# Attention beside a state-space scan on one core: some of the next unit's preparation steps move from between the scores to between the value products

## The chip, the cores and the metric

The kernel runs on one core of one Trainium2 chip (trn2). The metric is the device time of one execution in microseconds (us), the median of several runs. In the text PE is the matmul engine, DVE the vector engine, ACT the scalar engine, POOL the GpSimd engine and SP the queue that issues most DMAs. "Score" is q times k, "value product" is the weights times v.

## What is computed

One layer of a transformer that mixes attention with a state-space scan, for 2048 latent and 256 context tokens. The part that the change touches is the attention: 8 query heads on 2 key/value heads of size 64; latent queries attend to 2048 latent and 512 cached context keys, context queries to 256 keys.

```python
def block_attention(q, k, v):
    ...
    def one_block(q_blk):
        s = jnp.einsum("bqkgd,bskd->bkgqs", q_blk, k, preferred_element_type=jnp.float32) * scale
        p = jax.nn.softmax(s, axis=-1).astype(v.dtype)
        return jnp.einsum("bkgqs,bskd->bqkgd", p, v)
```

The state-space mixer (per direction a complex diagonal scan over the tokens) is independent of the attention; its work is put between the attention's instructions. Projections come before both, a gated projection and a feed-forward network after both.

## The kernel before

The attention is cut into **units**: one kv head, one pair of query heads, and 512 latent queries (16 latent units of 20 key blocks each) or 256 context queries (4 context units of 2 key blocks). A unit goes through its key blocks in **slots**, one for each block of 128 keys. In a slot, `scores` does four matmuls (L266, L267, two for each head, in the rounded format fp32r) and one exponential on ACT (L269). `values` does the value products of a slot (L283, two matmuls in full fp32, which the trace shows as four records) and adds p into a running sum for the denominators, on POOL (L296) or, for every fourth slot of a latent unit, the last of its group, on DVE (L293). Slots go in **groups of four**. `attend` writes the scores of group g+1 and then the values of group g, so PE alternates between a score phase (16 matmuls) and a value phase (16 records).

The exponential needs the row maximum of the scores beforehand. So while a unit runs, `prep` prepares the **next** one, as a generator whose every `yield` is one **step**: transposes of q (L218) and their split (L219, L222), then 40 maxima steps for a latent unit, each of one matmul (L197, 512 keys by 128 queries into one PSUM tile named `m`) and one reduction on DVE (L198, `mx<-m`); when a head's maxima are complete, a small reduction (L204), ACT and a transpose (L205, L210) put their negative into the operand `ql`. The tile `m` has three buffers, and everything that needs a scratch PSUM tile takes its turn on them: maxima, transposes, the denominators' sums (L317), the matmuls of the scan.

Inside `slot` the counter `st["q"]` grows by `st["per"]`, the steps still to do divided by 19.5, and a step is run for each whole number. In the windows of a latent unit whose successor is a latent unit `per` is 52 / 19.5 = 2.67, so two or three steps follow the scores of each slot. In the first three windows a context unit is prepared as well and `per` is 68 / 19.5 = 3.49.

After the values of a group come three things, in this order: a step of `finish` for a unit that has ended (among them an addition L312 and, one group on, the matmuls L317; another group on, the multiplication L335, which waits for a DMA), and one step of the generator `Sg`, which runs the scan. `Sg` also gets one step after the scores of each slot. Its five steps for a group mean that the scan's DVE work falls behind the values: per scan unit either three products and sums with the rotation table (L1032, L1033, L1034, here **s**), or the scan itself (L1040), or two products (L1047, L1048, here **r**), or one difference (L1052). The scan's matmuls (L1012, L982, L984, 48 short ones) fall into the score phase of about one group in five.

On PE and DVE the order of the program text is the order of execution: the attention is written inside

```python
    with tc.manual_schedule(engines={mybir.EngineType.PE, mybir.EngineType.DVE}):
        fin = attend(B, Sg)
```

The other engines and queues are ordered by the scheduler. The functions that the change touches, with the lines of the profile:

Of the kernel before, what the change touches and what calls it, by code (L numbers as in the profile page):

```python
# [48 lines left out]
def build(nc, tc, I, O):  # L49
# [76 lines left out]
    def run(g):  # L126
        for _ in g:
            pass
# [130 lines left out]
    def scores(ui, j):  # L259
        kv, tok, nq, k0, k1, pr_ = units[ui]  # L260
        khl, kho = KK[kv, k0]
        st = X["pst"].tile([128, 2, 512], F32, name="st")
        kc = slice(j * 128, (j + 1) * 128)
        for h in range(2):
            qh, ql = QT[ui][h]
            PE.matmul(st[:, h, 0:nq], khl[:, kc], qh[:, 0:nq], start=True, stop=False)  # L266
            PE.matmul(st[:, h, 0:nq], kho[:, kc], ql[:, 0:nq], start=False, stop=True)  # L267
        p = X["wk"].tile([128, 2, 512], F32, name="p", bufs=11)
        S.activation(p[:, :, 0:nq], st[:, :, 0:nq], AF.Exp, scale=0.125)  # L269
        pts[ui, j] = p  # L270
# [3 lines left out]
    def values(ui, j):  # L274
        kv, tok, nq, k0, k1, pr_ = units[ui]
        nk = k1 - k0
        if j == 0:
            PV[ui] = X["ppv"].tile([128, 512], F32, name="pv")
            ACC[ui] = {}
        pv, acc = PV[ui], ACC[ui]  # L280
        p = pts.pop((ui, j))
        for h in range(2):
            PE.matmul(pv[64 * h:64 * h + 64, 0:nq], X["vall"][:, k0 + j, 64 * kv:64 * kv + 64], p[:, h, 0:nq],  # L283
                      start=j == 0, stop=j == nk - 1)
        if nk <= 4:
            e = "v"
        elif ui + 1 == len(units):
            e = "v" if j % 3 == 2 or j > 16 else "g"
        else:
            e = "v" if j in VJ else "g"  # L290
        if e in acc:
            if e == "v":
                V.tensor_add(acc[e][:, :, 0:nq], acc[e][:, :, 0:nq], p[:, :, 0:nq])  # L293
            else:
                for h in range(2):
                    G.tensor_add(acc[e][:, h, 0:nq], acc[e][:, h, 0:nq], p[:, h, 0:nq])  # L296
        else:
            acc[e] = p
        if j == nk - 1:
            pvs = X["wk"].tile([128, 512], F32, name="pvs", bufs=2)  # L300
            S.copy(pvs[:, 0:nq], pv[:, 0:nq])
            PEND.append((ui, pvs, acc))
# [4 lines left out]
    def finish():  # L307
        ui, pvs, acc = PEND.pop(0)
        kv, tok, nq, k0, k1, pr_ = units[ui]
        a = acc["v"]  # L310
        if "g" in acc:
            V.tensor_add(a, a, acc["g"])  # L312
        if ui + 1 < len(units):
            yield
        sT = X["pmx"].tile([128, 512], F32, name="m")
        for h in range(2):
            PE.matmul(sT[64 * h:64 * h + 64, 0:nq], ones, a[:, h, 0:nq], start=True, stop=True)  # L317
        rT = X["wk"].tile([128, 512], F32, name="rT", bufs=2)
        if ui + 1 == len(units):
            V.reciprocal(rT[:, 0:nq], sT[:, 0:nq])  # L320
        else:
            S.copy(rT[:, 0:nq], sT[:, 0:nq])
            nc.sync.dma_start(out=rs_scr[ui, :, 0:nq], in_=rT[0:128:64, 0:nq])
            w = 2 * nq // 128
            rr = X["wk"].tile([128, 8], F32, name="rr", bufs=2)[:, 0:w]
            for h in range(2):
                nc.sync.dma_start(out=rr[64 * h:64 * h + 64], in_=rs_scr[ui, h, 0:nq].rearrange("(p w) -> p w", p=64))
            yield
            V.reciprocal(rr, rr)
            for h in range(2):  # L330
                nc.sync.dma_start(out=rr_scr[ui, h, 0:nq].rearrange("(p w) -> p w", p=64), in_=rr[64 * h:64 * h + 64])
            for h in range(2):
                nc.sync.dma_start(out=rT[64 * h:64 * h + 64, 0:nq], in_=rr_scr[ui, h:h + 1, 0:nq].to_broadcast([64, nq]))
        yield
        V.tensor_mul(pvs[:, 0:nq], pvs[:, 0:nq], rT[:, 0:nq])  # L335
        nc.sync.dma_start(out=a_scr[256 * kv + 128 * pr_:256 * kv + 128 * pr_ + 128, tok:tok + nq], in_=pvs[:, 0:nq])
# [3 lines left out]
    def prep_steps(ui):  # L340
        kv, tok, nq, k0, k1, pr_ = units[ui]
        n = 2 * (nq // 128) * ((k1 - k0 + 3) // 4) + 12
        first = next(i for i, u_ in enumerate(units) if (u_[0], u_[3]) == (kv, k0))
        return n + (1 + (k1 - k0 + 3) // 4 if ui == first else 0)

    def attend(B, Sg):
        groups = []
        for ui, u_ in enumerate(units):
            js = [(ui, j) for j in range(u_[4] - u_[3])]
            groups += [js[i:i + GROUP] for i in range(0, len(js), GROUP)]  # L350
        st = dict(ready=0, q=0.0, per=0.0, goal=1, s=0.0)
        fin = []

        def step():
            st["ready"] = next(B) or st["ready"]

        def slot(ui, j):
            while st["ready"] < ui:
                step()
            lat = units[ui][2] > 256  # L360
            if lat and not j:
                st["goal"] = min(ui + (2 if ui + 1 < 2 * len(cu) else 1), len(units) - 1)
                st["per"] = sum(prep_steps(i) for i in range(st["ready"] + 1, st["goal"] + 1)) / 19.5
                st["q"] = 0.0
            scores(ui, j)
            st["q"] += st["per"] if lat else 0.0
            while st["q"] >= 1.0:
                st["q"] -= 1.0
                if st["ready"] < st["goal"]:
                    step()  # L370
            if lat:
                X["pos"] = "p"
                next(Sg, None)

        for s_ in groups[0]:
            slot(*s_)
        for gi, g in enumerate(groups):
            if gi + 1 < len(groups):
                for s_ in groups[gi + 1]:
                    slot(*s_)  # L380
            for s_ in g:
                values(*s_)
            for f in list(fin):
                if next(f, "end") == "end":
                    fin.remove(f)
            if gi + 1 < len(groups) and len(groups[gi + 1]) > 2:
                X["pos"] = "v"
                next(Sg, None)
            if PEND:
                fin.append(finish())  # L390
        run(Sg)
        return fin
# [754 lines left out]
    with tc.manual_schedule(engines={mybir.EngineType.PE, mybir.EngineType.DVE}):  # L1147
        fin = attend(B, Sg)
# [569 lines left out]
```

## Time and profile before

| what | value |
|---|---|
| median of 3 runs | 3324.7 us (3320.79 to 3324.88) |
| the profiled execution's own time | 3312.73 us |
| its span, from first to last instruction | 3310.9 us |
| PE busy | 92% of the span |
| DVE busy | 77% |
| POOL busy | 57% |
| ACT busy | 41% |
| latent attention, from 476.88 us to 1419.73 us | 942.85 us |

A busy PE is not a PE at its peak: the ends of its matmuls are modelled, and waits that are shorter than a matmul's tail do not show as idle time. What a wait costs is therefore read from the starts of neighbouring matmuls. Times inside the trace are counted from the span's start.

### The profile page before, as it was taken

What the parts mean: (1) busy time and instruction counts of PE and PEld (TensorE: products, weight loads), DVE (VectorE), ACT (ScalarE), POOL (GpSimd) and SP (SyncE); (2) the same over time, 40 slices, a digit from 0 to 9 for tenths busy, and PEclk for the clock granted to TensorE, in tenths of its full rate; (3) what the DMA queues carried; (4) which work ended last, traced back from release to release, by engine and by line L of the source; (5) the groups of instructions that cost most, each with busy time, mean ns of one, the idle gap of its engine ahead of it and who ended that gap; (6) DMA issues with size and microseconds to landing.
All of it is one profiled execution on the core that took longest, in us unless ns stands there. A gap on an engine that the chain in (4) does not pass through costs nothing. (4 is left out here: it accounts for less than half of the span.)

```text
span 3310.9 us, 46264 instructions
## 1 busy us (share of the span) xinstructions
PE 3059.0 (92%) x16087; PEld 2468.7 (75%) x16087; DVE 2547.8 (77%) x3444; ACT 1341.8 (41%) x2378; POOL 1888.8 (57%) x1373
## 2 busy tenths in 40 slices
PE   7898889999999999996997999999999999989897
PEld 5787665555655565565776999999989998868686
DVE  4899766777777787667878877887787877577887
ACT  4333334444444444544555333443343334232332
POOL 3777526655775785774435544554455555354675
PEclk9999999999999999998998999999999999999899
DMA  7565452323333322214565444444434445658653
GB/s 264 181 198 191 145 133 55 89 71 87 85 81 90 81 75 52 65 60 138 184 184 184 134 120 121 129 136 118 121 106 130 122 127 185 155 151 198 179 199 137
DMA packets 515379, 435.19 MB, mean 131 GB/s; under 512 B 106374, under 2 KB 449454, under 8 KB 515148
## 3 DMA queue, kind: packets, MB, share of 16 engines
q1 hardware_dynamic: 498060, 400.57, 40.1%
q0 software_dynamic: 5184, 18.88, 3.3%
q10 hardware_dynamic: 11904, 12.82, 1.2%
q8 instruction: 127, 2.08, 0.3%
q14 instruction: 104, 0.85, 0.1%
HBM read 279.37 MB, written 143.73 MB: 128 GB/s over the span
## 5 line engine op out<-in xcount | busy, mean ns | idle before, releaser
L296 POOL TENSOR_TENSOR p<-p 128x512 f32<-128x512 f32 x442 | 647.0, 1502 | 286.7 <-PE pv L283 185.7
L89 POOL TENSOR_TENSOR op<-wr,op 128x512 fp32r<-128x512 f32 (+1 forms) x297 | 416.4, 1409 | 413.5 <-ACT op L88 373.9
L95 PE MATMUL o<-h,op 128*128 128x384 f32 x1848 | 621.3, 336 | 18.3 <-DVE h L89 17.2
L94 PE MATMUL o<-h,op 128*128 128x384 f32 x1848 | 621.0, 336 | 16.4 <-ACT h L88 15.8
L96 PE MATMUL o<-h,op 128*128 128x384 f32 x1848 | 620.2, 336 | 0.0
L198 DVE TENSOR_REDUCE mx<-m 128x1 f32<-128x512 f32 (+1 forms) x656 | 404.8, 675 | 134.6 <-PE m L197 133.3
L269 ACT ACTIVATE p<-st 128x1024 f32<-128x1024 f32 (+1 forms) x328 | 331.4, 1016 | 245.5 <-PE st L267 236.3
L88 ACT CAST op<-sw 128x512 fp32r<-128x512 f32 (+1 forms) x381 | 232.5, 612 | 328.7 <-PE o L95 257.0
L95 PEld LDWEIGHTS o<-h,op 128*128 128x128 f32 x1848 | 349.2, 189 | 20.8 <-DVE h L89 19.3
L94 PEld LDWEIGHTS o<-h,op 128*128 128x128 f32 x1848 | 349.0, 189 | 18.2 <-ACT h L88 17.2
L96 PEld LDWEIGHTS o<-h,op 128*128 128x128 f32 x1848 | 349.2, 189 | 0.0
L89 POOL TENSOR_TENSOR op<-sw,op 128x512 fp32r<-128x512 f32 (+1 forms) x177 | 259.4, 1469 | 118.4 <-ACT op L88 118.3
L88 ACT CAST op<-wr 128x512 fp32r<-128x512 f32 (+1 forms) x333 | 198.9, 607 | 244.7 <-PE o L95 162.7
L283 PE MATMUL pv<-p,vall 128*64 128x512 f32 (+1 forms) x1312 | 296.4, 593 | 0.0
L95 PE MATMUL o<-fvm,op 128*128 128x512 f32 x693 | 277.7, 401 | 19.9 <-POOL fvm L89 10.5
L94 PE MATMUL o<-fvm,op 128*128 128x512 f32 x693 | 276.7, 400 | 11.3 <-ACT fvm L88 9.6
L266 PE MATMUL st<-qh,khl 128*128 128x512 f32 (+1 forms) x656 | 277.6, 424 | 9.8 <-ACT p L269 8.8
L96 PE MATMUL o<-fvm,op 128*128 128x512 f32 x693 | 274.4, 396 | 0.0
L267 PE MATMUL st<-ql,kho 128*128 128x512 f32 (+1 forms) x656 | 259.4, 396 | 0.0
L197 PE MATMUL m<-khl,qh 128*128 128x512 f32 (+1 forms) x656 | 230.0, 422 | 30.5 <-DVE mx L198 20.2
L283 PEld LDWEIGHTS pv<-p,vall 128*64 128x64 f32 x1312 | 86.8, 136 | 158.2 <-issue 155.0
L197 PEld LDWEIGHTS m<-khl,qh 128*128 128x128 f32 x656 | 124.3, 191 | 103.5 <-DVE mx L198 67.7
(314 smaller groups left out, 6302.2 us busy)
## 6 DMA issues: line engine op xcount, KB each, us to landing
wr<-w_ffn_in SPq DMA_DIRECT2D x132, 512.0 KB
wm<-w_mod SPq DMA_DIRECT2D x48, 512.0 KB
act_scr<-s SPq DMA_DIRECT2D x99, 192.0 KB
wr<-act_scr SPq DMA_DIRECT2D x36, 512.0 KB
x_scr<-gy POOLq DMA_DIRECT2D x36, 512.0 KB, 6.0
xt<-x SPq DMA_DIRECT2D x34, 512.0 KB
act_scr<-gy SPq DMA_DIRECT2D x90, 192.0 KB
sw<-act_scr SPq DMA_DIRECT2D x54, 256.0 KB
```

Source lines behind the costliest of these rows:

```text
L88: a = (copy or S.copy)(hi, src)
L89: b = (sub or V).tensor_sub(lo, src, hi.bitcast(F32))
L94: PE.matmul(out, ah, bh, start=first, stop=False)
L95: PE.matmul(out, ah, bl, start=False, stop=False)
L96: return PE.matmul(out, al, bh, start=False, stop=last)
L197: PE.matmul(sp_[:, 0:b - a], qh[:, i * 128:(i + 1) * 128], khl[:, a:b], start=True, stop=True)
L198: V.tensor_reduce(mxs[h][:, i, c:c + 1], sp_[:, 0:b - a], axis=AX.X, op=ALU.max)
L266: PE.matmul(st[:, h, 0:nq], khl[:, kc], qh[:, 0:nq], start=True, stop=False)
L267: PE.matmul(st[:, h, 0:nq], kho[:, kc], ql[:, 0:nq], start=False, stop=True)
L269: S.activation(p[:, :, 0:nq], st[:, :, 0:nq], AF.Exp, scale=0.125)
L283: PE.matmul(pv[64 * h:64 * h + 64, 0:nq], X["vall"][:, k0 + j, 64 * kv:64 * kv + 64], p[:, h, 0:nq], start=j == 0, stop=j == nk - 1)
L296: G.tensor_add(acc[e][:, h, 0:nq], acc[e][:, h, 0:nq], p[:, h, 0:nq])
```

## The change

In `slot` a latent slot now counts 0.75 of `per`. The rest is counted in the loop over a group's values: after the second and after the fourth value product of a group of four, half of `per` each, so that one value phase gets 1 `per` and one score phase 3. The loop that runs the steps becomes a function, `steps`.

```diff
+        def steps(n):
+            st["q"] += n
+            while st["q"] >= 1.0:
+                st["q"] -= 1.0
+                if st["ready"] < st["goal"]:
+                    step()
+
         def slot(ui, j):
...
             scores(ui, j)
-            st["q"] += st["per"] if lat else 0.0
-            while st["q"] >= 1.0:
-                st["q"] -= 1.0
-                if st["ready"] < st["goal"]:
-                    step()
+            steps(0.75 * st["per"] if lat else 0.0)
             if lat:
                 X["pos"] = "p"
                 next(Sg, None)
...
-            for s_ in g:
+            for i, s_ in enumerate(g):
                 values(*s_)
+                if len(g) > 2 and i % 2:
+                    steps(0.5 * st["per"])
             for f in list(fin):
```

Instruction counts stay as they are; the order on PE and DVE changes, from the first latent unit to the one before the last. The line numbers after the change are larger by 5 behind this place (the scan's L1052 becomes L1057).

The first place is on DVE, in the unit that runs from 1118 us to 1178 us: from the end of its first score phase to the first maxima of its third. `mx<-m` are the maxima, `p<-p` of L293 is the denominators' sum of a group, `p<-p` of L312 that of the unit before, `r<-r,rw` the scan's difference, and `s`, `sw` its three products and sums. Before:

```order
L198 TENSOR_REDUCE mx<-m 128x1 x5
L293 TENSOR_TENSOR p<-p 128x1024
L1052 TENSOR_TENSOR r<-r,rw 128x584
L198 TENSOR_REDUCE mx<-m 128x1 x11
L312 TENSOR_TENSOR p<-p 128x1024
L1032 TENSOR_TENSOR s<-s,et 128x584
L1033 SCALAR_TENSOR_TENSOR sw<-sw,sg,et 128x584
L1034 TENSOR_TENSOR s<-s,sw 128x584
L198 TENSOR_REDUCE mx<-m 128x1 x4
```

The same place after the change:

```order
L198 TENSOR_REDUCE mx<-m 128x1 x4
L293 TENSOR_TENSOR p<-p 128x1024
L198 TENSOR_REDUCE mx<-m 128x1
L1057 TENSOR_TENSOR r<-r,rw 128x584
L198 TENSOR_REDUCE mx<-m 128x1 x11
L312 TENSOR_TENSOR p<-p 128x1024
L1037 TENSOR_TENSOR s<-s,et 128x584
L1038 SCALAR_TENSOR_TENSOR sw<-sw,sg,et 128x584
L1039 TENSOR_TENSOR s<-s,sw 128x584
L198 TENSOR_REDUCE mx<-m 128x1 x4
```

One maximum has moved behind the sum L293 and stands ahead of the scan's difference. Of the 11 maxima that follow, 8 belong to the score phase now and 3 to the value phase, and these 3 still stand ahead of the sum L312 and the scan's s.

The second place is on PE at the same point of the program: the value phase of the first group and the first slot behind it. `pv` are the value products (eight matmuls for a group), `st` the scores, `m<-khl,qh` the matmul of a maximum. Before:

```order
L283 MATMUL pv<-p,vall 64x512 x8
L266 MATMUL st<-qh_512_10088,khl_0_8962 128x512
L267 MATMUL st<-ql_512_10089,kho_0_8963 128x512
L266 MATMUL st<-qh_512_10105,khl_0_8962 128x512
L267 MATMUL st<-ql_512_10106,kho_0_8963 128x512
L197 MATMUL m<-khl_0_8962,qh_512_10579 128x512 x2
```

After the change:

```order
L283 MATMUL pv<-p,vall 64x512 x4
L197 MATMUL m<-khl_0_8962,qh_512_10579 128x512
L283 MATMUL pv<-p,vall 64x512 x4
L197 MATMUL m<-khl_0_8962,qh_512_10579 128x512 x2
L266 MATMUL st<-qh_512_10088,khl_0_8962 128x512
L267 MATMUL st<-ql_512_10089,kho_0_8963 128x512
L266 MATMUL st<-qh_512_10105,khl_0_8962 128x512
L267 MATMUL st<-ql_512_10106,kho_0_8963 128x512
L197 MATMUL m<-khl_0_8962,qh_512_10579 128x512 x2
```

The value products are cut in two by one maximum, and two more maxima stand between the last value product and the next score. The transposes L210 that end a unit's preparation change places too: they stood ahead of the unit's last value phase but one and now stand behind it, directly ahead of the next unit's first scores.

## Rows read from the trace of the kernel before

**Rows 1.** Busy time by windows, latent attention: window, length, each engine's busy time, clock, DMA.
```profile
476.88:1419.73 942.85, 892.91 (x4147) 540.04 (x4145) 706.61 (x912) 427.44 (x674) 623.60 (x431) 0.99 0.29 77
```
**Rows 2.** Waits in that window: who waits for whom, us, times, longest.
```profile
DVE mx L198 <- PE m L197: 129.4, 86, 4.7
PEld m L197 <- DVE mx L198: 60.6, 128, 3.6
PE m L197 <- DVE mx L198: 15.9, 27, 3.2
```
**Rows 3.** Windows, one unit's ten phases: PE, PEld, DVE, ACT, POOL, clock, DMA.
```profile
1118.21:1124.81 6.60, 6.50 (x31) 4.64 (x30) 4.81 (x6) 4.92 (x6) 4.17 (x3) 1.00 0.32 83
1124.81:1128.39 3.58, 3.58 (x17) 1.06 (x16) 3.11 (x5) 0.40 (x1) 0.00 (x0) 1.00 0.93 160
1128.39:1142.47 14.08, 13.10 (x77) 10.77 (x76) 7.96 (x12) 6.60 (x14) 0.00 (x0) 1.00 0.24 65
1142.47:1146.05 3.58, 3.58 (x17) 1.06 (x16) 3.25 (x4) 0.40 (x1) 2.36 (x2) 1.00 0.14 30
1146.05:1152.85 6.80, 6.53 (x28) 4.65 (x27) 5.22 (x10) 3.44 (x5) 6.80 (x6) 1.00 0.44 134
1152.85:1157.29 4.44, 4.44 (x21) 1.34 (x20) 4.44 (x4) 0.76 (x1) 4.44 (x4) 1.00 0.38 93
1157.29:1164.15 6.86, 6.86 (x33) 5.04 (x31) 5.36 (x9) 5.09 (x8) 6.86 (x6) 1.00 0.21 47
1164.15:1167.73 3.58, 3.58 (x17) 1.06 (x16) 3.58 (x6) 0.31 (x1) 3.58 (x3) 1.00 0.00 0
1167.73:1174.81 7.08, 5.72 (x27) 4.02 (x25) 7.05 (x8) 3.81 (x5) 7.08 (x6) 1.00 0.36 81
1174.81:1178.39 3.58, 3.58 (x17) 1.05 (x16) 3.19 (x3) 0.85 (x2) 3.58 (x3) 1.00 0.41 112
```
**Rows 4.** Timeline of DVE about that unit's second value phase: start, length, idle before.
```profile
1141.37 1.21 DVE L312 TENSOR_TENSOR p<-p 128x1024 f32<-128x1024 f32 x1
1142.50 0.76 DVE L1032 TENSOR_TENSOR s<-s,et 128x584 f32<-128x584 f32 x1
...
1144.03 1.72 DVE L1034 TENSOR_TENSOR s<-s,sw 128x584 f32<-128x584 f32 x1
1147.52 2.65 DVE L198 TENSOR_REDUCE mx<-m 128x1 f32<-128x512 f32 x4 [1.77 <-PE m L197]
```
**Rows 5.** Timeline of DVE, the scan's s in the unit before.
```profile
1094.06 1.83 DVE L1032 TENSOR_TENSOR s<-s,et 128x584 f32<-128x584 f32 x1
...
1097.67 1.73 DVE L1034 TENSOR_TENSOR s<-s,sw 128x584 f32<-128x584 f32 x1
```
**Rows 6.** Timelines of DVE, then PE, about the score phase at 1263.53.
```profile
1261.19 2.32 DVE L312 TENSOR_TENSOR p<-p 128x1024 f32<-128x1024 f32 x1
1263.43 1.85 DVE L1047 TENSOR_TENSOR r<-r,et 128x584 f32<-128x584 f32 x1
1265.20 1.85 DVE L1048 SCALAR_TENSOR_TENSOR rw<-rw,sg,et 128x584 f32<-128x584 f32 x1
1266.98 2.47 DVE L198 TENSOR_REDUCE mx<-m 128x1 f32<-128x512 f32 x4
...
1265.93 0.39 PE L197 MATMUL m<-khl,qh 128*128 128x512 f32 x1
1267.71 1.10 PE L197 MATMUL m<-khl,qh 128*128 128x512 f32 x2 [1.39 <-DVE mx L198]
```
**Rows 7.** Windows of that score phase: until the clock falls, and from there on.
```profile
1263.53:1269.60 6.07, 4.58 (x20) 3.24 (x19) 6.04 (x8) 2.05 (x2) 6.07 (x5) 1.00 0.00 0
1269.60:1273.35 3.75, 3.75 (x10) 2.44 (x9) 2.61 (x6) 1.63 (x3) 3.75 (x4) 0.54 0.02 4
```
**Rows 8.** Timeline of PE, two maxima ahead of a value phase.
```profile
899.72 0.62 PE L197 MATMUL m<-khl,qh 128*128 128x512 f32 x2
900.27 3.65 PE L283 MATMUL pv<-p,vall 128*64 128x512 f32 x16
```

## The prediction, made before the changed kernel was timed

> **What bounds the kernel now.** I read the window of the latent attention first, then the waits in it, then one unit phase by phase, and last the timelines at the places where PE or DVE stands. In 942.85 us of latent attention PE is busy 892.91 us, DVE 706.61 and POOL 623.60 [rows 1]. PE sets the time, but DVE is close behind it: the matmul of a maximum waits for DVE to empty a tile `m` for 60.6 us (at its weight load) and 15.9 us (at the matmul itself), and DVE waits for a maximum's matmul for 129.4 us in 86 pieces [rows 2]. So both wait for each other by turns, and an order decides who waits.
>
> The unit from 1118.21 us shows the turns [rows 3]. Call its phases S1, V1, S2, V2, ... S5, V5, in the order of the rows. The reader should see two things. First, DVE is busy in value phases already (3.11 of 3.58, 3.25 of 3.58, 4.44 of 4.44, 3.58 of 3.58, 3.19 of 3.58), although no maximum is computed there: it finishes the last two maxima and then does the sums and the scan's work. Secondly, its slack lies at the start of the score phases: in S3 it starts its first maximum 1.47 us into the phase, after 1.77 us of idleness [rows 4], because the deferred work (L312, then s) had ended 0.3 us ahead of S3 (1144.03 + 1.72 against 1146.05). The value phases are the time in which DVE clears what is not a maximum.
>
> A late DVE costs PE time at one point. Three tiles `m` let PE run three maxima ahead; the fourth waits until DVE has read the first. At 1263.53 this can be seen [rows 6]: L312 and r keep DVE until 1267.05, the first maximum is read from 1266.98, and PE's fourth maximum starts at 1267.71, 0.7 us behind that, after 1.39 us of idleness. That phase took 6.07 + 3.75 = 9.82 us [rows 7], the phase with the same ten maxima and an early DVE 6.80 [rows 3].
>
> **The change part by part.** It removes and adds no work; it moves maxima. In a window with `per` 2.67 the maxima of the five score phases go from 5, 11, 10, 10, 4 to 3, 8, 8, 7, 4, and the value phases get 1+1, 1+2, 1+1, 2+1 and none (the first number behind the second value product, the other behind the fourth). No DMA is moved but the load of q at the start of a unit, which stays in the first slot.
>
> *Price on PE.* Maxima start 0.23 us apart (two in 0.62 us [rows 8], one 0.39 [rows 6]); a value product starts 0.32 us behind the last maximum (900.27 less 899.72 less 0.23 [rows 8]), 0.09 more than another maximum would. Both sides of a cut may pay that, so a cut costs 0.1 to 0.3 us; I take 0.2. V1 and V2 so become 4.2 and 4.5 us, V3 and V4 5.1 and 4.5, and the score phases lose 0.23 for each maximum taken out.
>
> *Price on DVE.* A maximum takes 0.6 us there (four in 2.47 [rows 6]); DVE reads it about 0.5 us after its matmul starts (1.47 less four scores at 0.23 [rows 4]). In V2 the first moved maximum starts on PE at 1.8 us and is read until 2.9; the next two start at 3.9 and 4.1 and are read from 4.4 to 5.6. L312 and s stand behind them and can't start before. Today L312 runs at the end of S2, and s from the start of V2 [rows 4]. So DVE stands idle under the value products, waiting for PE, with work of its own in the queue: that is the step on which the prediction rests.
>
> L312 takes 1.21 us where POOL is idle (S2, POOL 0.00 [rows 3, 4]) and 2.32 where it is busy [rows 6]; s takes 3.25 us so (1142.50 to 1145.75 [rows 4]) and 5.34 so (1094.06 to 1099.40 [rows 5]). POOL is busy from the last 2.36 us of V2 on and all through S3 [rows 3], where both would now lie: I take 2.3 and 5.3. The Trainium skill's page SBUF — State Buffer, section Who interferes with whom, says that a DVE instruction with two inputs in SBUF contends with GpSimd's reads and a reduction never does; the trace agrees, with 1.21 against 2.32 for L312. By the uncontended rows S3 would be 3.2 us shorter than below.
>
> Then DVE is free at 5.6 + 2.3 + 5.3 = 13.2 us of V2, which is 8.7 us into S3. PE does four scores, two maxima, four scores, one maximum (2.6 us) and stands until 8.7 + 0.7 = 9.4; behind that are left five maxima and eight scores, 3.0 us. S3 lasts 12.2 to 12.4 us instead of 6.80: +5.4.
>
> The other phases of this unit, in the same way. S1: two maxima fewer and their wait, -0.65. V1 +0.65. S2: three maxima fewer (0.7), and the scan's matmuls, which take their turn on the same three tiles, now follow two maxima and not three; PE idles 0.98 us there (14.08 less 13.10 [rows 3]); -2.0 in all (0.7 to 2.5). V2 +0.9, V3 +0.65. S4: behind V3 stand L293 (sized as L312: 2.3) and the scan L1040, which I take at L312's 2.3 for want of a row (1.2 to 5.3); DVE is free 3.0 us into S4, whose fourth maximum comes at 4.0: no wait, -0.85. V4 +0.9. S5: two maxima until 3.5, L293 until 5.8, one maximum, r 3.6 (1263.43 to 1267.05 [rows 6]) until 10.0, which is 5.5 into S5; fourth maximum at 6.2, then nine matmuls: 8.3 instead of 7.08, +1.2. V5: the transposes of L210 move here from S5, and the first scores of the next unit wait for their copy, for which nothing else is in between: 0 to 1.5 us (the hand-over from PE to DVE of rows 4 as the upper end), taken +0.7 with the transposes. Sum: -0.65 + 0.65 - 2.0 + 0.9 + 5.4 + 0.65 - 0.85 + 0.9 + 1.2 + 0.7 = **+6.9 us** on the unit's 60.2.
>
> The scan's cycle is a little longer than a unit, so units come in four kinds, by what stands behind V2 and V4. Behind V2: s (above), r (3.6), the difference (1.8), the scan (2.3); with 5.6 + 2.3 - 4.5 = 3.4 us ahead of them, PE's fourth maximum in S3 waits 5.1, 3.3 and 3.8 us. Less two maxima and the waits that these phases have today (up to 1.39 [rows 6]) that is +3.5, +2.3, +2.5. Behind V4: s costs S5 about +2.9, the scan and the difference nothing. With the same small terms: about +6, +3.5, +3.5. Mean of the four kinds 5.0. Eleven windows are of this pattern (of 12 with a `per` of 2.67, the last has no scan work): **+55**. The first three windows move maxima out of phases that have 13 or 14, where DVE itself sets the pace; what it loses under the values it saves at the start of the scores: 0 (-2 to +3 each).
>
> *The clock.* Behind the idleness of 1.39 us the granted clock fell to 0.54, its lower level (1.2 GHz) for nearly all of 3.75 us, while PE had work [rows 7]; 3.4 us at half speed lose 1.7. With 128 waits in rows 2 this is rare, so I count it for every second late phase, one such phase in a window: 11 x 0.5 x 1.7 = +9.
>
> Sum: +64 us on the profiled execution's 3312.73, so 3377. That execution lies 12 us under the median of the three runs; on the median, 3324.7 + 64 = **3389 us**. Nothing behind the attention waits for anything else that could take it up.
>
> **Rivals.** *The waits go away (faster).* If the deferred work were over by about 1.9 us into the score phases, as with DVE's uncontended prices in V1, PE would stand nowhere: the matmuls' waits of 60.6 + 15.9 us bound the gain, less 60 cuts at 0.2. Half of that net 64 gives -32: 3293. For it speaks that DVE idles 129.4 us in these phases' starts; against it that V3 and V4 have no idle DVE into which three maxima (1.8 us) could go [rows 3]. It decides at the place of L312 and s: a deferred work of under 2 us behind V2.
>
> *The change moves the waits and no more.* What S3 and S5 lose, S2 and S4 give back; 3325, within 6 us.
>
> *The clock goes with it.* Every wait of 1.4 us or longer is followed by a stretch at the lower level, as in rows 7, and late phases cost what that one did, 9.82 - 6.80 = 3.0 us more: on top of the 55 come 11 x 3 = 33, and 12 in the first windows: 3324.7 + 55 + 33 + 12 = 3425. The Trainium skill's page TensorE: Matmul & The Clock Gate, section HAM oscillation, says that a PE that idles between bursts starts each burst at the low clock; the row at 1269.60 agrees, while most of the 128 waits are short.
>
> **How the numbers follow.** Forecast 0.55, clock 0.20, no more than moved 0.12, faster 0.13. Around the forecast the prices of L312 and s (3.2 us in one window of four, similar in S5), the cuts (0.1 to 0.3) and the first windows (-6 to +9) make 3350 to 3410. The range goes from 3318, which leaves out the faster case, to 3425. A difference under 0.2% (6.6 us) is not to be told from none here; slower by more than that 0.80 (forecast, clock and 0.05 of the moved case), within it 0.07, faster 0.13.
>
> **What would show it.** Right: in the changed trace the L312 and the scan's instructions start 4 to 6 us behind the start of their value phase, with DVE idle ahead of the moved maxima; the longest waits of L197 for L198 go from 3.6 us to over 5 us, in S3 and S5; S2 and S1 get shorter; value phases of 4.2 to 5.1 us; some more stretches at the lower clock between 742 us and the end of the attention. Wrong: waits of L197 for L198 that shrink in total, S3 under 7 us, or an unchanged attention of 943 us.

## The result, and the profile after

The change made the kernel **slower: 3359.4 us against 3322.7 us** (medians of four runs each beside one another), a ratio of 1.0133 with an interval of 1.0110 to 1.0156. The profiled executions differ by 48.7 us (3361.45 against 3312.73), their spans by 47.0, and 44.8 of that lies in the window of [rows 1]. The same part of the program in the changed kernel:

```profile
478.07:1465.74 987.67, 911.25 (x4146) 545.95 (x4145) 673.41 (x913) 427.95 (x673) 601.52 (x432) 0.97 0.28 73
```

PE's share falls from 0.947 (892.91 of 942.85) to 0.923, DVE's from 0.749 to 0.682, and the granted clock from 0.99 to 0.97. So neither engine became the bound; both wait more. The waits of [rows 2] after:

```profile
DVE mx L198 <- PE m L197: 201.7, 158, 4.1
PEld m L197 <- DVE mx L198: 126.8, 113, 6.2
PE m L197 <- DVE mx L198: 60.4, 34, 5.8
```

All three grew: DVE waits for a maximum's matmul 201.7 us instead of 129.4, and the weight load of a maximum for DVE 126.8 us instead of 60.6. The third line is no further loss: all but 0.1 us of its 60.4, the waits at the matmul itself, lie inside the 126.8. The unit of [rows 3], phase by phase:

```profile
1141.88:1147.60 5.72, 5.72 (x31) 4.20 (x29) 5.01 (x6) 4.75 (x7) 4.29 (x3) 1.00 0.31 84
1147.60:1152.10 4.50, 4.50 (x20) 1.45 (x19) 3.02 (x5) 0.96 (x2) 0.00 (x0) 1.00 1.00 201
1152.10:1163.60 11.50, 11.50 (x74) 10.33 (x72) 6.43 (x10) 6.62 (x15) 0.00 (x0) 1.00 0.30 77
1163.60:1168.32 4.72, 4.72 (x20) 1.64 (x20) 0.72 (x2) 0.40 (x1) 3.50 (x3) 1.00 0.14 29
1168.32:1182.62 14.30, 8.53 (x26) 6.01 (x24) 11.94 (x14) 3.92 (x5) 14.30 (x11) 0.77 0.32 93
1182.62:1188.31 5.69, 5.69 (x23) 1.61 (x22) 3.72 (x6) 0.27 (x1) 5.48 (x4) 0.98 0.00 0
1188.31:1194.22 5.91, 5.91 (x29) 4.63 (x27) 4.46 (x7) 4.72 (x8) 4.57 (x4) 1.00 0.25 55
1194.22:1198.96 4.74, 4.74 (x21) 1.56 (x21) 3.50 (x5) 0.74 (x1) 4.08 (x4) 1.00 0.00 0
1198.96:1204.38 5.42, 4.93 (x21) 3.49 (x19) 5.38 (x11) 2.77 (x3) 3.12 (x3) 1.00 0.28 70
1204.38:1208.38 4.00, 4.00 (x21) 1.48 (x21) 3.67 (x3) 1.32 (x3) 4.00 (x3) 1.00 0.49 122
```

66.50 us instead of 60.18. Look at the fourth and the fifth row. In V2 DVE works 0.72 us of 4.72, where it worked 3.25 of 3.58; in S3 PE works 8.53 of 14.30. The timeline of DVE from the start of V2 on (start, length, what, and in brackets the idleness ahead of it) has the reason:

```profile
1166.00 0.69 DVE L198 TENSOR_REDUCE mx<-m 128x1 f32<-128x512 f32 x1 [3.20 <-PE m L197]
1168.29 1.29 DVE L198 TENSOR_REDUCE mx<-m 128x1 f32<-128x512 f32 x2 [1.60 <-PE m L197]
1169.50 1.39 DVE L312 TENSOR_TENSOR p<-p 128x1024 f32<-128x1024 f32 x1
1170.81 1.82 DVE L1037 TENSOR_TENSOR s<-s,et 128x584 f32<-128x584 f32 x1
1172.56 1.82 DVE L1038 SCALAR_TENSOR_TENSOR sw<-sw,sg,et 128x584 f32<-128x584 f32 x1
1174.41 1.71 DVE L1039 TENSOR_TENSOR s<-s,sw 128x584 f32<-128x584 f32 x1
1176.04 2.47 DVE L198 TENSOR_REDUCE mx<-m 128x1 f32<-128x512 f32 x4
```

DVE stands for 3.20 us (2.40 of them in V2, which starts at 1163.60) and 1.60 us, waiting for a moved maximum, while L312 and s are in its queue behind it. When they run it is S3, and PE's maxima of S3 are not read before 1176.04. On PE, in the same trace:

```profile
1169.25 0.62 PE L197 MATMUL m<-khl,qh 128*128 128x512 f32 x2
...
1170.61 0.39 PE L197 MATMUL m<-khl,qh 128*128 128x512 f32 x1
1176.77 0.79 PE L197 MATMUL m<-khl,qh 128*128 128x512 f32 x1 [5.78 <-DVE mx L198]
1177.37 0.63 PE L266 MATMUL st<-qh,khl 128*128 128x512 f32 x1
```

Three maxima fill the three tiles `m`, the fourth waits 5.78 us, and from there on a matmul takes 0.63 instead of 0.39 us, since the clock has fallen. The windows of S3, cut at 1175.00 (granted clock third from the right; 0.57 is the lower level, 1.2 GHz, for most of the stretch):

```profile
1168.32:1175.00 6.68, 2.68 (x12) 1.88 (x10) 6.65 (x6) 2.05 (x2) 6.68 (x5) 1.00 0.45 140
1175.00:1182.62 7.62, 5.85 (x14) 4.13 (x14) 5.30 (x9) 1.87 (x3) 7.62 (x7) 0.57 0.21 51
```

### The profile page after: what moved, and what is told of

Read it like the earlier page. It is cut to its first block, busy times and chain, and to the rows that moved or that the text cites. A ratio compares the mean times of both kernels' runs of the same rounds, so it can differ in the third digit from the quotient of the medians.

```text
span 3357.9 us, 46269 instructions
## 1 busy us (share of the span) xinstructions
PE 3085.0 (92%) x16087; PEld 2479.0 (74%) x16087; DVE 2519.4 (75%) x3444; ACT 1343.3 (40%) x2378; POOL 1861.8 (55%) x1373
## 5 line engine op out<-in xcount | busy, mean ns | idle before, releaser
L296 POOL TENSOR_TENSOR p<-p 128x512 f32<-128x512 f32 x442 | 624.7, 1451 | 331.5 <-PE pv L283 169.4
L198 DVE TENSOR_REDUCE mx<-m 128x1 f32<-128x512 f32 (+1 forms) x656 | 415.2, 676 | 209.9 <-PE m L197 205.8
L197 PE MATMUL m<-khl,qh 128*128 128x512 f32 (+1 forms) x656 | 248.6, 435 | 68.0 <-DVE mx L198 64.7
L283 PE MATMUL pv<-p,vall 128*64 128x512 f32 (+1 forms) x1312 | 309.7, 598 | 0.0
L266 PE MATMUL st<-qh,khl 128*128 128x512 f32 (+1 forms) x656 | 279.2, 426 | 2.6 <-ACT p L269 1.8
L197 PEld LDWEIGHTS m<-khl,qh 128*128 128x128 f32 x656 | 125.7, 196 | 201.2 <-DVE mx L198 133.9
L267 PE MATMUL st<-ql,kho 128*128 128x512 f32 (+1 forms) x656 | 267.0, 408 | 5.6 <-ACT ql L211 5.6
L89 DVE TENSOR_TENSOR op<-sw,op 128x512 fp32r<-128x512 f32 (+1 forms) x204 | 204.2, 1001 | 0.8 <-ACT op L88 0.7
```

The costliest lines, as they stand in the source:

```text
L89: b = (sub or V).tensor_sub(lo, src, hi.bitcast(F32))
L197: PE.matmul(sp_[:, 0:b - a], qh[:, i * 128:(i + 1) * 128], khl[:, a:b], start=True, stop=True)
L198: V.tensor_reduce(mxs[h][:, i, c:c + 1], sp_[:, 0:b - a], axis=AX.X, op=ALU.max)
```

## Experiments

All ratios are to the kernel before, run on the same chip beside each. Theory: the moved maxima stand ahead of the deferred work (the step of `finish` and the scan's step) on in-order DVE, and make it late. First rival: the cut itself (fp32r maxima between fp32 value products) costs what was lost. The table is a ledger of the profiled executions that goes with all of them. "S" and "V" are the sums of the 79 score phases with 16 scores and the 78 value phases with 16 records from the start of the window on, a phase being from the first L266 to the first L283 and back again; "clock" is (1 - mean granted clock) times the length of the latent attention, the mean taken over 180 equal windows of it; it is an upper bound of what the clock took, since idle time is in it.

| kernel | ratio (interval) | S, us | V, us | clock, us |
|---|---|---|---|---|
| before | 1 | 679.9 | 295.0 | 10.3 |
| the change | 1.0133 (1.0110 to 1.0156) | 650.4 | 368.3 | 28.9 |
| e1, all behind the second | 1.0073 (1.0052 to 1.0094) | 625.2 | 365.5 | 13.7 |
| e2, all behind the fourth | 1.0136 (1.0115 to 1.0158) | 665.0 | 355.7 | 34.1 |
| e3, half behind deferred work | 1.0104 (1.0085 to 1.0123) | 647.2 | 363.8 | 23.8 |
| e4, deferred work first | 0.9941 (0.9923 to 0.9958) | 584.8 | 365.4 | 6.8 |
| f0, before with one more matmul | 1.0101 (1.0077 to 1.0126) | 659.7 | 338.6 | 0.0 |
| f1, before, deferred work first | 1.0006 (0.9992 to 1.0020) | 678.1 | 295.1 | 6.9 |
| f2, e4 without a cut | 0.9926 (0.9907 to 0.9944) | 598.5 | 349.6 | 8.6 |
| f3, e4 with half moved | 1.0120 (1.0101 to 1.0140) | 544.5 | 471.2 | 39.2 |
| g1, only the scan's step first | 0.9933 (0.9914 to 0.9952) | 574.0 | 368.6 | 1.7 |
| g2, only finish's step first | 1.0092 (1.0074 to 1.0109) | 640.2 | 364.2 | 23.9 |
| g3, f2 with half as many moved | 0.9935 (0.9918 to 0.9953) | 629.6 | 323.4 | 10.2 |

The change moves 145 maxima into value phases. At 0.23 us that is 33.4 us from S to V. V grew by 73.3, so 39.9 are the price of cuts and of what else has moved there: 72 of the transposes L210 stand in value phases instead of 8, and 16 of L218, while the granted clock is below 1 for next to nothing of V (0.1 us lost). S fell by 29.5 and not by 33.4. This alone looks like the cut's doing. The experiments show that it isn't: S could have fallen much further.

**e1, the whole `per` behind the second value product.**

```diff
-                if len(g) > 2 and i % 2:
-                    steps(0.5 * st["per"])
+                if len(g) > 2 and i == 1:
+                    steps(1.0 * st["per"])
```

> The kernel after, with the whole 1.0 per of a value phase behind the second value product and none behind the fourth. Theory (the moved maxima hold up the deferred work on the in-order DVE): the maxima are matmuls at about 1.8 to 2.3 us of the value phase and read until about 4.1 instead of 5.6, so what stands behind them starts 1.5 us earlier; the late score phase of the unit at 1142 us goes from 14.29 us to 12 to 13, and the ratio to the kernel before from 1.0133 to 1.006 to 1.010. Rival (the cut itself, fp32r maxima between fp32 value products, costs what was lost): the cut in the middle stays, 1.011 to 1.013, and the late score phase keeps its 14 us.

1.0073, in the theory's range. V is nearly as long as in the change (the middle cut is still there), S is 25.2 us shorter. DVE in V2 and S3 of the same unit:

```profile
1149.22 1.89 DVE L198 TENSOR_REDUCE mx<-m 128x1 f32<-128x512 f32 x3 [3.20 <-PE m L197]
1151.02 1.82 DVE L312 TENSOR_TENSOR p<-p 128x1024 f32<-128x1024 f32 x1
1152.77 1.85 DVE L1037 TENSOR_TENSOR s<-s,et 128x584 f32<-128x584 f32 x1
```

V2 starts at 1146.82 there, so L312 starts 4.20 us behind it instead of 5.90 (1169.50 less 1163.60), and S3 lasts 12.1 us instead of 14.3.

**e2, the whole `per` behind the fourth.** The same edit with `i == 3`.

> The kernel after, with the whole 1.0 per behind the fourth value product, so that no value phase is cut in two. Theory: the maxima are read at 4.1 to 5.9 us of the value phase, no earlier than now, and the deferred work is as late: ratio 1.010 to 1.015, the late score phase of the unit at 1142 us 13 to 15 us, and DVE's idleness ahead of a maximum at least the 201.7 us of the kernel after. Rival (the cut): the loss goes away, 0.997 to 1.003.

1.0136, as the theory has it, and against the rival: without a cut in the middle V is 12.6 us shorter, but S is 14.6 longer, since the maxima are read no sooner (L312 starts 5.92 us behind the start of V2, S3 lasts 13.9 us). DVE's idleness ahead of a maximum was to be at least 201.7 us; it is 196.5.

**e3, half of the moved maxima behind the deferred work.**

```diff
-                if len(g) > 2 and i % 2:
+                if len(g) > 2 and i == 1:
                     steps(0.5 * st["per"])
...
                 next(Sg, None)
+            if len(g) > 2:
+                steps(0.5 * st["per"])
```

> The kernel after, with half of per behind the second value product and the other half behind the step of finish and the scan's step, so that one or two maxima a group go behind the deferred work instead of ahead of it. Theory: the deferred work starts at about 2.9 us of the value phase instead of 5.6, the late score phase of the unit at 1142 us falls to 10 to 12 us, and the ratio to 1.003 to 1.009. Rival (the cut, which stays in the middle and at the end): 1.012 to 1.014.

1.0104 lies between the two ranges, and S3 lasts 12.5 us, a little over the theory's 10 to 12. The deferred work does start earlier, L312 3.0 us behind the start of V2, but one maximum still stands ahead of it, behind 3.19 us of idleness:

```profile
1169.35 0.69 DVE L198 TENSOR_REDUCE mx<-m 128x1 f32<-128x512 f32 x1 [3.19 <-PE m L197]
1169.96 1.79 DVE L312 TENSOR_TENSOR p<-p 128x1024 f32<-128x1024 f32 x1
```

The maxima that went behind the deferred work then fill two of the three tiles at the end of V2, so PE's wait begins after the first slot of S3. That second effect I had left out of the expectation.

**e4, the deferred work first.** It goes behind the second value product, ahead of every moved maximum; the maxima stay where the change put them.

```diff
+            def deferred():
+                ...
             for i, s_ in enumerate(g):
                 values(*s_)
                 if len(g) > 2 and i % 2:
+                    if i == 1:
+                        deferred()
                     steps(0.5 * st["per"])
-            for f in list(fin):
-                ...
-            if gi + 1 < len(groups) and len(groups[gi + 1]) > 2:
-                X["pos"] = "v"
-                next(Sg, None)
+            if len(g) <= 2:
+                deferred()
```

`deferred()` holds the lines that are taken out below.

> The kernel after, with the step of finish and the scan's step written behind the second value product, ahead of the two halves of per: all maxima of the value phase stand behind the deferred work. Theory: DVE starts the deferred work under the value products as in the kernel before; PE can wait only for the three tiles that the moved maxima fill, so the late score phase of the unit at 1142 us falls to 7 to 10 us, and the ratio to 0.995 to 1.004. Rival (the cut, still made twice in a phase): 1.010 to 1.014.

0.9941, a little under the theory's range: with the same maxima behind the same value products, and nearly the same cuts (V 365.4 against 368.3; only the matmuls L317 of a `finish` move with their step), the loss becomes a gain, because S is 65.6 us shorter. S3 took 5.56 us, less than the theory's 7 to 10:

```profile
1128.46:1134.02 5.56, 5.56 (x26) 4.32 (x24) 5.33 (x10) 3.45 (x5) 5.56 (x5) 1.00 0.36 101
```

That is little more than the bare starts of its 24 matmuls at 0.23 us (5.52). DVE at that place, V2 from 1123.74 to 1128.46:

```profile
1122.86 1.22 DVE L312 TENSOR_TENSOR p<-p 128x1024 f32<-128x1024 f32 x1
1123.99 0.76 DVE L1043 TENSOR_TENSOR s<-s,et 128x584 f32<-128x584 f32 x1
1124.67 0.82 DVE L1044 SCALAR_TENSOR_TENSOR sw<-sw,sg,et 128x584 f32<-128x584 f32 x1
1125.52 1.72 DVE L1045 TENSOR_TENSOR s<-s,sw 128x584 f32<-128x584 f32 x1
1127.17 0.68 DVE L198 TENSOR_REDUCE mx<-m 128x1 f32<-128x512 f32 x1
1128.43 4.03 DVE L198 TENSOR_REDUCE mx<-m 128x1 f32<-128x512 f32 x6 [0.58 <-PE m L197]
```

s ends at 1127.24, before the value phase does. It also takes 3.25 us instead of 5.31: its first two parts, 0.76 and 0.82 us, lie before or at the beginning of the 3.51 us that POOL works in this phase. The waits of the latent attention in that trace:

```profile
DVE mx L198 <- PE m L197: 100.3, 105, 2.4
PEld m L197 <- DVE mx L198: 68.8, 92, 2.6
PE m L197 <- DVE mx L198: 19.1, 20, 2.2
```

The weight loads of the maxima wait for DVE 68.8 us instead of the change's 126.8, in no piece longer than 2.6. That is no less than before (60.6), so these waits aren't what e4 gains over the kernel before. Of the 95.1 us that S lost, 33.4 are the matmuls that moved; the weight loads of the scan's matmuls L1012 and L982 waited 25.1 us for DVE before and 7.1 here; where the rest lies was not parted.

**f0, the price of a cut by itself.** The kernel before, with a matmul that nothing reads.

```diff
+                if i == 1 and gi + 1 < len(groups) and len(groups[gi + 1]) > 2:
+                    un = groups[gi + 1][-1][0]
+                    kv, _, _, k0, _, _ = units[un]
+                    dm = X["pmx"].tile([128, 512], F32, name="m")
+                    PE.matmul(dm, QT[un][0][0][:, 0:128], KK[kv, k0][0][:, 0:512], start=True, stop=True)
```

> The kernel before, with one more matmul of the maxima's form behind the second value product wherever a latent score phase stands ahead of the value phase (about 78 times), into a tile m that nothing reads. It prices a cut by itself, with DVE's order unchanged. Theory (a cut costs about 0.23 us beside the matmul's 0.23, as value phases of 4.73 and 4.50 us show, and the late scores come from DVE's order): value phases of 3.58 us become 4.0 to 4.1, ratio 1.007 to 1.012. Rival (the cuts alone account for the 44.8 us of the change, 0.7 to 0.8 us each): value phases of 4.5 us and more, ratio 1.018 to 1.026.

1.0101, the theory's; a value phase takes a little more than its 4.0 to 4.1 us. The timeline of PE at one:

```profile
1157.92 1.94 PE L283 MATMUL pv<-p,vall 128*64 128x512 f32 x8
1159.79 0.50 PE L387 MATMUL m<-khl,qh 128*128 128x512 f32 x1
1160.22 1.94 PE L283 MATMUL pv<-p,vall 128*64 128x512 f32 x8
1162.09 0.50 PE L266 MATMUL st<-qh,khl 128*128 128x512 f32 x1
```

4.17 us instead of 3.58 (1157.92 to 1162.09): 0.59 for the matmul and the cut, 0.36 of it the cut. A single maximum at the end of a value phase costs less: value phases with one there and no cut took 3.92 us in g3, 0.34 more than 3.58, or 0.11 beside the matmul. With both, two or three moved maxima make 4.51 and 4.74 (3.58 + 0.59 + 0.34, and 0.23 more), and the trace of the change has 4.50 and 4.72. The change has maxima in 58 value phases, so pairs of cuts at 0.47 cost up to 27 us there. That is a price on V alone: in f0 V grew by 43.6 us, but S shrank by 20.2 with no maximum moved. What gave this back (the clock, 10.3 us at most, or the time that DVE gains while a longer value phase runs) was not parted.

**f1, the deferred work first and no maximum moved.** The edit of e4 to the kernel before.

> The kernel before, no maximum moved, with the step of finish and the scan's step written behind the second value product. It parts the gain of the kernel in which both were moved (0.9941). Theory: with no maxima in the value phases the deferred work is first in DVE's queue already, so its place there changes nothing, 0.997 to 1.003; the gain of 0.9941 needs the moved maxima. Rival (the earlier deferred work alone brings the gain): 0.991 to 0.996.

1.0006: nothing. The place of the deferred work matters only where maxima stand ahead of it, and the gain of e4 comes from the moved maxima.

**f2, e4 without the cut**: `deferred()` behind the second, `steps(1.0 * st["per"])` behind the fourth.

> The deferred work behind the second value product, and all of the 1.0 per behind the fourth, so no value phase is cut in two. Theory: a cut costs 0.2 us or a little more, about 55 of them go away, and DVE has the deferred work to do until then in any case: 0.988 to 0.993, score phases as in the kernel with 0.9941. Rival (DVE needs the early maxima to be busy under the value products, or PE waits in the score phase for tiles filled late): 0.995 to 1.001.

0.9926, not to be told from 0.9941. V is 15.8 us shorter than in e4, S 13.7 longer: both the theory's saving and the rival's loss are there, and nearly cancel, as between e2 and the change.

**f3, e4 with half of the maxima moved**: 0.5 of `per` in a slot and 1.0 behind the second and the fourth value product.

> The kernel with 0.9941, with 0.5 of per in a slot instead of 0.75, and 1.0 per instead of 0.5 behind the second and the fourth value product, so that half of the maxima lie under the value products. Theory: five or six maxima at 0.6 us beside a deferred work of 1.8 to 5.5 us overfill a value phase of 5.4 us, what is over holds up the score phases and takes the rest of the gain: 0.995 to 1.010. Rival (there was slack left under the value products, the gain goes on): 0.985 to 0.993.

1.0120, slower than the range of the theory. The 317 maxima moved should bring V to 368 (0.23 each), and cuts at 0.47 in 60 phases to 396; it is 471.2. Nine value phases with seven maxima in them took 9.4 us on average, twice a full one of e4 (4.72): three tiles and a busy DVE hold PE up inside the value phase too, with waits of L197 for L198 of up to 4.13 us there. All nine lie in the first three windows. The lower clock is part of it (39.2 us in the table, 14.9 of them in V).

**g1 and g2, which part of the deferred work it is.** The edit of e4, with only the scan's step (g1) or only the step of `finish` (g2) moved ahead.

> The kernel with 0.9941, but only the scan's step stands behind the second value product, ahead of the moved maxima; the step of finish (L312 and others) is back behind all of them. Theory: the scan's sums are the larger part of what was late (5.3 of the 6.7 us in the late phase at 1168 us), so most of the loss goes: ratio 0.995 to 1.002, the s phase 6 to 8 us. Rival (L312, which is first in the queue, is what holds DVE up): 1.007 to 1.012.

> The kernel with 0.9941, but only the step of finish stands behind the second value product; the scan's step is back behind the moved maxima. Theory: L312 takes 1.2 to 1.4 us of the late phase, once in a unit, and the scan's step is as late as in the change: 1.005 to 1.012, the s phase 12 to 13.5 us. Rival (L312 is what holds DVE up): 0.994 to 0.999.

The scan's step alone brings all of it (0.9933, more than the theory's 0.995 to 1.002), the step of `finish` takes away about a third of the loss (1.0092 against 1.0133). The two parts of the unit that carry it, V2 and S3, in g1 and then in g2:

```profile
1110.38:1115.11 4.73, 4.73 (x21) 1.64 (x20) 2.52 (x5) 0.40 (x1) 3.52 (x3) 1.00 0.13 27
1115.11:1121.99 6.88, 5.85 (x26) 4.25 (x24) 6.84 (x11) 3.52 (x5) 6.88 (x6) 1.00 0.50 156
```

```profile
1160.11:1164.84 4.73, 4.73 (x21) 1.64 (x20) 1.06 (x3) 0.40 (x1) 3.51 (x3) 1.00 0.13 27
1164.84:1175.86 11.02, 7.45 (x25) 5.40 (x23) 9.53 (x13) 3.52 (x5) 11.02 (x9) 0.85 0.41 120
```

The second row of each is S3: 6.88 us as expected, and 11.02, a little under the 12 to 13.5 expected of g2.

**g3, an eighth moved instead of a quarter**: f2 with 0.875 of `per` in a slot and 0.5 behind the fourth.

> The kernel without a cut (0.9926), with half as many maxima moved: 0.875 of per in a slot and 0.5 behind the fourth value product. Theory (the gain is work of DVE put into time in which it was idle, so it goes with the number moved until the value phase is full): 0.995 to 0.998. Rival (a quarter was already too much, and an eighth loses less in waits and cuts): 0.987 to 0.992.

0.9935, under the theory's range and above the rival's: it is as fast as f2 within the intervals. The gain is flat from 74 to 145 moved maxima and turns into a loss at 317 (f3). That it would go with the number was wrong.

e4, f2, g1 and g3 all beat the kernel before by 0.6 to 0.7%; their intervals overlap, and which is best stays open.

## Why the prediction was right, and which terms were off

**The mechanism was right.** The step on which the prediction rested, that DVE stands idle under the value products with work of its own in the queue, is in the trace of the change (3.20 and 1.60 us of idleness, then L312 and s), and e4 takes it away and the loss with it. The longest waits are in S3, as predicted (6.2 us; over 5 was said), though not in S5 as well (2.6 at most); S1 and S2 got shorter, value phases took 4.00 to 5.69 us (4.2 to 5.1 was said). In the unit the sum was +6.9, and +6.3 was measured. That closeness is luck: S3 was priced 2.1 us too low and S5 2.9 too high. The whole was too high: +64 was forecast, and the medians differ by 36.7 us, the profiled executions by 48.7.

The rival "the waits go away" has its condition, deferred work over by about 1.9 us into the score phase, in e4, where it is over before S3 begins (in g1 L312 ends 3.05 us into S3, at 1118.16). Its price counted one wait twice: PE's 15.9 us lie inside the 60.6 of the weight loads, so half of 60.6 less the cuts' 12 is 24 us and not 32, a ratio of 0.993 where e4 has 0.9941. But the waits that it was to remove are still there in e4, 68.8 us, so that the number agrees is luck.

**Term by term in that unit**, predicted and measured: S1 -0.65, -0.88; V1 +0.65, +0.92; S2 -2.0, -2.58; V2 +0.9, +1.14; S3 +5.4, +7.50; V3 +0.65, +1.25; S4 -0.85, -0.95; V4 +0.9, +1.16; S5 +1.2, -1.66; V5 +0.7, +0.42.

- *S3 was sized too small, by the clock.* The wait was even a little shorter than worked out: PE's fourth maximum starts 8.45 us into S3 (9.4 predicted), because L312 took 1.39 us and not 2.3; s took 5.31, as predicted (5.3). But what follows lasts 5.85 us instead of 3.0, at a clock of 0.57. The Trainium skill's page TensorE: Matmul & The Clock Gate, section HAM oscillation, which stood beside the clock rival, describes this: idleness, then work at the low clock.
- *S5 was wrong in sign.* r and L293 were priced at their contended lengths (3.6 and 2.3). In the trace POOL is busy for only 3.12 of 5.42 us there, r's two parts take 0.7 and 0.8 us, and L293 takes 1.55 us, most of it in V4 (it starts at 1197.84, S5 at 1198.96); so DVE isn't late, and the phase loses a part of the wait that it had before (PE 5.72 of 7.08 [rows 3], 4.93 of 5.42 here):

```profile
1197.84 1.55 DVE L293 TENSOR_TENSOR p<-p 128x1024 f32<-128x1024 f32 x1
...
1200.02 0.71 DVE L1052 TENSOR_TENSOR r<-r,et 128x584 f32<-128x584 f32 x1
1200.65 0.81 DVE L1053 SCALAR_TENSOR_TENSOR rw<-rw,sg,et 128x584 f32<-128x584 f32 x1
```

- *The cuts were sized a little small*: 0.36 + 0.11 a pair against 0.2 twice.

**The mean over the kinds was too high.** The first three windows were to stay, and did: 207.73 us (469.28 to 677.01) against 208.59. The eleven windows of the pattern were to cost +55 and the clock +9; together they cost +44.8. Their window in the changed kernel:

```profile
677.01:1411.57 734.56, 675.32 (x3096) 410.72 (x3094) 505.44 (x661) 317.25 (x501) 446.79 (x319) 0.97 0.28 75
```

against 689.79 us in the kernel before (676.47 to 1366.26). Eight of the eleven grew by 2.8 to 8.0 us, but three got shorter. Two of these are of the kind in which the scan's matmuls fall into S3 itself, forecast at +3.5. In the one from 1055.13 us S3 was 13.26 us and is 13.43, while S1, which held 3.21 us of PE's waiting for ACT, went from 11.00 to 6.20. I had carried the small terms of one unit over to the other kinds without looking at their own phases. The clock went the other way: by the table it took up to 18.6 us more, twice the +9. There are 14 stretches at the lower level where there were five. The rival "the clock goes with it" had every wait of 1.4 us or longer followed by one, and this did not come: of 22 such waits of PE in the changed latent attention, eight (1.43 to 2.21 us) were not. The windows behind a wait of 2.20 us and behind one of 2.17:

```profile
719.51:722.68 3.17, 3.17 (x13) 2.36 (x13) 2.63 (x5) 1.37 (x2) 3.17 (x4) 1.00 0.63 173
804.04:807.84 3.80, 3.80 (x10) 2.79 (x10) 3.77 (x5) 1.02 (x1) 2.94 (x4) 0.56 0.75 221
```

What decides between the two was not tried. In sum the +64 held one term that was too high and one that was too low, and the range held the result because its width came from other terms.

That the cut alone explains the loss is ruled out by e2 (no cut, no gain) and e4 (nearly the same cuts, a gain); that it has a share is not: by f0's price it is up to 27 us of the +73.3 of V.

## What to carry to other kernels

On an in-order engine ask of every instruction that is moved forward what then stands behind it: an instruction that must wait for another engine belongs behind the engine's own ready work, even if its slot looked idle. If the order is right, a small shift already gives what there is (an eighth did as much as a quarter here), and too large a one fills the buffers between the engines and loses more than it gains. Price each kind of window from its own rows, and add the clock to every wait of several microseconds.

## What the runs showed of the hardware that was not expected

*More work, a higher clock.* f0 has 80 matmuls more, 75 of them in the 78 value phases of the table, and in its one profiled execution the mean granted clock of the latent attention is 1.000 in all 180 windows, while seven are below 0.95 in the kernel before. So part of the price of its matmuls can be paid back by the clock (10.3 us at most, by the table). That the matmul itself is the cause was not tried; its waits are shorter too (the longest of L197 for L198 is 2.5 us instead of 3.6).

*An addition of DVE that took 12.79 us.* In the trace of e3 one L293 took over five times its usual 1.2 to 2.3 us and made PE wait 11.45 us. Beside it POOL, at work without a gap since 699.78, ran its additions at 1.23 us each instead of the 1.46 us of their mean:

```profile
706.49 12.79 DVE L293 TENSOR_TENSOR p<-p 128x1024 f32<-128x1024 f32 x1
...
708.33 9.87 POOL L296 TENSOR_TENSOR p<-p 128x512 f32<-128x512 f32 x8
```

It ended 1.08 us behind the last of them (706.49 + 12.79 against 708.33 + 9.87). f0 has one such case (7.18 us) and f3 one (9.66), in each case until POOL's row of additions ended; in the other profiles the longest L293 is 3.41 us. The Trainium skill's page SBUF — State Buffer, section Who interferes with whom, calls the ports that the two share an exclusive lock and says that the order of issue decides who blocks. The rows agree in that an instruction of POOL was running when L293 started, in all three cases; but L293 stayed blocked behind more than that one, here behind eight L296 in a row. What decides between this and the usual 1.2 to 2.3 us was not tried.
